# Layer 0 of a hybrid decoder trunk: the core's outputs are turned by VectorE in squares of 32 and put in place through DRAM

## The chip, the cores and the metric

The kernel runs on one core of a Trainium2 chip. The time is the device time of one execution in microseconds (us), the median of several runs. A profile of one execution gives the span from the first to the last instruction and every instruction's start, duration and waits.

## The reference

The kernel computes two layers of a decoder trunk on 1024 tokens of width 1024. Layer 0 is gated linear attention (GLA) in four heads, layer 1 is sparse attention. The change touches layer 0 alone. Its mixer, cut to what matters here:

```python
h = x @ w_in                                  # q, k, v, z, and the gate's low-rank input a
g = log_sigmoid(a @ w_a2 + b_a) / 16
...
o = o_intra + o_inter                         # within a chunk, and from the state S
o = o * rsqrt(mean(o * o, axis=-1) + 1e-5)    # per token and head, over 512 values
o = o.reshape(B, L, 2048) * gn_g
y = (o * silu(z)) @ w_out
...
x = layer_norm(ALPHA * x + y)                 # then a gated embedding is added
```

## The kernel before

**Halves, heads, chunks.** Layer 0 runs in two halves of 512 tokens; each half runs the four heads one after the other, and each head (a dictionary `u`, a "unit" of the planner) works in four chunks of 128 tokens. So there are 32 chunks with an output `o`. For each head the kernel makes the values (`v_phase`), queries and keys (`qk_phase`), and then the core: `core_steps` gives 16 steps, four for each chunk. `s1` makes the scores of a chunk and turns its keys, `s2` brings the state `R` forward, `s3` makes the chunk's output of three matmuls (with a state nine) in the PSUM bank `o`, and `s4` turns that output and gates it. Beside the core's steps run the bulk phases: the output projection of the head before (`out_phase`) and the gate projection of the next head (`z_phase`). The last head of a half has no z phase beside it, and its own output projection follows at once.

**Precision.** Matmuls are in fp32r with every operand split into a high and a low part: ScalarE writes the high part (`whi`, `uh`, L189 and L418), VectorE subtracts it from the value (`wlo`, `ul`, L191, L193 and L410). A product takes three matmuls of 512 columns. That goes for weights too, which come from DRAM into `wst` (L209) and are split up to two blocks ahead of their use (`Weights.step`).

**The turn.** `o` stands with tokens on the partitions (128 x 512). The output projection needs the head's 512 channels on the partitions, in four blocks `b` of 128, with the tokens along the row. In `s3`, VectorE copies `o` out of PSUM into `ot` (L729) and ScalarE sums its squares into `ss` (L731). In `s4`, TensorE turns the four 128 x 128 blocks of `ot` against an identity (L747, recorded at L62) into the PSUM bank `oT`, VectorE multiplies that by the gate `z` into `uf` (L757), and the product is split into `uh` and `ul` (L418, L410). GpSimd (POOL) makes the normalising factor `rs` of the chunk (L753, L755), which the projection's accumulation into `y` applies (L784).

**The order of the work.** The program is written out by a planner (`Flow`). It keeps a clock `now` that advances with each matmul it writes (512 columns count 0.213 us, a transpose 0.109 us), and a heap of jobs with due times on this clock: `after(dt, f)` puts one in, `chain` puts several behind each other, `spread` spaces a list evenly. A job that lacks something (`fl.req`) is put back by 0.3 us. `fl.need` runs jobs ahead of their times until a condition holds. The clock sets only the order in which instructions are written to each engine's queue; on the chip, each engine works through its queue in order and waits on semaphores. `spread(steps, fl.now, n * B + 15.5)` spaces a core's 16 steps, where `B` is 5.12 us and `n` the number of bulk blocks beside it: 8 for heads 1 and 2, and 4 for heads 0 and 3.

**Who waits for u.** `out_phase` takes `u["u"][t]` of its chunk `t` by `fl.need`, in the order of the chunks, with 12 matmuls on each. In heads 0 to 2 this is after the next head's `v_phase` and `qk_phase`; in head 3 it follows the core. `u["prev"]["out"]` counts the chunks that the previous head's projection has finished, after which their buffers `u` may be used again.

**The DMA queue.** All transfers are issued by SyncE (SP) from one queue, in the order written: weight loads (L209), and in the background, the weights of layer 1, which are loaded, split and stored in DRAM ahead of their use (`split_ahead`: L223, L235, L239, one step each 2.06 us of the planner's clock). In the other layer, `attend` already turns squares of 32 on VectorE (L1512), stores them in DRAM by four transfers (L1525) and loads them back (L1535).

Of the kernel before, what the change touches and what calls it, by code (L numbers as in the profile page):

```python
# [10 lines left out]
F32 = mybir.dt.float32  # L11
F32R = mybir.dt.float32r
# [4 lines left out]
AF = mybir.ActivationFunctionType  # L17
OP = mybir.AluOpType
# [7 lines left out]
GH = 4  # L26
ALPHA = 4.0 ** 0.25
EPS = 1e-5
# [19 lines left out]
class Flow:  # L48
# [20 lines left out]
    def after(self, dt, fn):  # L69
        self.at(self.now + dt, fn)  # L70

    def chain(self, *steps):

        (_, first), rest = steps[0], steps[1:]
        first()
        if rest:
            self.after(rest[0][0], lambda: self.chain((0, rest[0][1]), *rest[1:]))
# [200 lines left out]
def trunk_kernel(ctx, tc, x_tok, x_T, p_T, pos, freq, g_q, g_k, g_v, g_z, g_a, g_a2, g_ba, g_gn, g_o,  # L278
                 d_q, d_k, d_v, d_z, d_qi, d_ki, d_o, ln_gb, ple_c, gate_c, out):
    nc = tc.nc  # L280
    act, dve, pool = nc.scalar, nc.vector, nc.gpsimd
    fl = Flow(nc)
    mm, after, chain = fl.mm, fl.after, fl.chain
# [4 lines left out]
    dp = ctx.enter_context(tc.tile_pool(name="dp", bufs=1, space=bass.MemoryType.DRAM))  # L288
# [6 lines left out]
    lp = open_pool(layer0, "lp")  # L295
# [116 lines left out]
    def split(hi, lo, src, done=None):  # L412

        def second():
            lo_part(lo, src, hi)
            if done:
                done()
        chain((0, lambda: act.activation(hi, src, AF.Copy)), (0.9, second))  # L418
# [60 lines left out]
    def t2k(tag, dt=F32, bufs=8):  # L479
        return lp.tile([128, 512], dt, tag=tag, name=tag, bufs=bufs)  # L480
# [147 lines left out]
    def core_steps(u):  # L628
        h, half = u["h"], u["half"]
        fl.need(lambda: "qhl" in u and "D" in u)  # L630
        q, k, Dt, v = u["q"], u["k"], u["D"], u["v"]
        qh, ql = u["qhl"]
        u["ss"] = cp.tile([128, 4], F32, tag="ss", name="ss", bufs=2)
        u["rs"] = cp.tile([128, 4], F32, tag="rs", name="rs", bufs=2)
        st = {}

        def has_state(c):
            return not (half == 0 and c == 0)

        def makes_state(c):  # L640
            return not (u["last"] and c == 3)

        def make_S(c):
            parts = [[lp.tile([128, 512], F32R, tag=f"S{n}{d}", name="S") for n in "hl"] for d in range(2)]

            def high(d):
                return lambda: act.activation(parts[d][0], R[h][:, d], AF.Copy, scale=Dt[:, d, c:c + 1])

            def low(d):
                def f():  # L650
                    dve.scalar_tensor_tensor(parts[d][1], R[h][:, d], Dt[:, d, c:c + 1], parts[d][0].bitcast(F32),
                                             op0=OP.mult, op1=OP.subtract)
                    if d:
                        st["S", c] = parts
                        st["made", c] = True
                return f

            chain((0, high(0)), (0.6, high(1)), (0.5, low(0)), (0.6, low(1)))

        def s1(c):  # L660
            def f():
                cs = slice(c * 128, c * 128 + 128)
                if c == 0 and half:
                    make_S(0)
                tr = pp.tile([128, 4, 128], F32, tag="tr", name="tr")
                for d in range(2):
                    mm(tr[:, 0], k[:, d, cs], q[:, d, cs], d == 0, d == 1)
                if makes_state(c):
                    for d in range(2):
                        fl.transpose(tr[:, 1 + d], k[:, d, cs], ident)  # L670
                Af = Afs[c % 2]
                Ah = lp.tile([128, 128], F32R, tag="Ah", name="Ah", bufs=2)
                Al = lp.tile([128, 128], F32R, tag="Al", name="Al", bufs=2)
                kh = lp.tile([128, 2, 128], F32R, tag="kh", name="kh")
                kl = lp.tile([128, 2, 128], F32R, tag="kl", name="kl")

                def a():
                    dve.copy_predicated(Af, cmask, tr[:, 0])
                    if makes_state(c):
                        act.activation(kh, tr[:, 1:3], AF.Copy)  # L680

                def b():
                    if makes_state(c):
                        lo_part(kl, tr[:, 1:3], kh)
                        st["kt", c] = kh, kl
                    act.activation(Ah, Af, AF.Copy)

                def d_():
                    lo_part(Al, Af, Ah)
                    st["A", c] = Ah, Al  # L690
                    st["At", c] = fl.now
                chain((0, a), (0.6, b), (0.7, d_))
            return f

        def s2(c):
            def f():
                if not makes_state(c):
                    return
                fl.req(("kt", c) in st, v[c] is not None, not has_state(c) or ("made", c) in st)
                kh, kl = st.pop(("kt", c))  # L700
                vh, vl = v[c]
                for d in range(2):
                    ps = pp.tile([128, 512], F32, tag="U", name="U", bufs=2)
                    mm(ps, kh[:, d], vh, True, False)
                    mm(ps, kh[:, d], vl, False, False)
                    mm(ps, kl[:, d], vh, False, True)
                    if has_state(c):
                        dve.scalar_tensor_tensor(R[h][:, d], R[h][:, d], Dt[:, d, c:c + 1], ps,
                                                 op0=OP.mult, op1=OP.add)
                    else:  # L710
                        dve.tensor_copy(R[h][:, d], ps)
            return f

        def s3(c):
            def f():
                cs = slice(c * 128, c * 128 + 128)
                fl.req(("A", c) in st, v[c] is not None, not has_state(c) or ("S", c) in st)
                fl.ripe(st["At", c] + 1.6)
                Ah, Al = st.pop(("A", c))
                vh, vl = v[c]  # L720
                ps = pp.tile([128, 512], F32, tag="o", name="o")
                ops = [(Ah, vh), (Al, vh), (Ah, vl)]
                if has_state(c):
                    for d, (sh, sl) in enumerate(st.pop(("S", c))):
                        ops += [(qh[:, d, cs], sh), (ql[:, d, cs], sh), (qh[:, d, cs], sl)]
                for i, (l, r) in enumerate(ops):
                    mm(ps, l, r, i == 0, i == len(ops) - 1)
                ot = lp.tile([128, 512], F32, tag="ot", name="ot", bufs=2)
                dve.tensor_copy(ot, ps)  # L729
                junk = lp.tile([128, 512], BF16, tag="junk", name="junk")  # L730
                act.activation(junk, ps, AF.Square, accum_out=u["ss"][:, c:c + 1])  # L731
                st["o", c] = ot
                st["ot", c] = fl.now
                u["late"] = c == 3
                if c < 3:
                    after(0.3, lambda: make_S(c + 1))
            return f

        def s4(c):
            def f():  # L740
                cs = slice(c * 128, c * 128 + 128)
                fl.req(("o", c) in st, "z" in u, h == 0 or u["prev"].get("out", 0) > c)
                fl.ripe(st["ot", c] + 1.1)
                ot = st.pop(("o", c))
                ps = pp.tile([128, 4, 128], F32, tag="oT", name="oT")
                for b in range(4):
                    fl.transpose(ps[:, b], ot[:, b * 128:b * 128 + 128], ident)  # L747
                uf = lp.tile([128, 4, 128], F32, tag="uf", name="uf", bufs=2)
                uh, ul = t2k("u", F32R), t2k("u", F32R)

                def done():
                    rc = slice(c, c + 1)
                    pool.tensor_scalar(u["rs"][:, rc], u["ss"][:, rc], ALPHA ** 2 / 512.0, ALPHA ** 2 * EPS,  # L753
                                       op0=OP.mult, op1=OP.add)
                    pool.tensor_tensor(u["rs"][:, rc], u["rs"][:, rc], mhalf[:, rc], op=OP.pow)  # L755
                    u["u"][c] = uh, ul
                chain((0, lambda: dve.tensor_mul(uf, ps, u["z"][:, :, cs])),  # L757
                      (0.8, lambda: split(uh, ul, uf.rearrange("p b t -> p (b t)"), done)))
            return f

        return fl.ordered([s1(0), s2(0), s3(0), s1(1), s4(0), s2(1), s3(1), s1(2), s4(1), s2(2), s3(2), s1(3), s4(2),
                           s2(3), s3(3), s4(3)])

# [1075 lines left out]
```

## Time and profile before

| | |
|---|---|
| Median of 3 runs | 1962.26 us (1962.2 to 1963.73) |
| Span of the profiled execution | 1962.1 us |
| Instructions | 26826 |
| Layer 0, about | 0 to 1020 us |
| Copies of `o` out of PSUM (L729) | 32, from 88.3 to 940.0 us |
| Transposes of `ot` on TensorE | 128, from 92.2 to 941.4 us |
| Gate products (L757) | 32, from 94.2 to 941.8 us |

The profiled execution's own time isn't listed apart from the runs; its span lies 0.2 us below their median. The profile's engines are PE (TensorE's matmuls), PEld (its weight loads, which overlap the matmuls), DVE (VectorE), ACT (ScalarE), POOL (GpSimd) and SP. `out<-in` names the tiles that an instruction writes and reads. A line such as L58 or L410 can be a helper's, so groups are told apart by tiles. `<-` behind an idle time names what ended it. The chain of work that ended last is followed back from the last instruction; an engine that fills the chain sets the time.

### The profile page before, as it was taken

How to read it: one execution, taken by the hardware profiler on the slowest of the kernel's cores; microseconds unless marked ns; L12 is line 12 of the kernel's file. 1: busy time of each engine (PE TensorE's matmuls, PEld its weight loads, DVE VectorE, ACT ScalarE, POOL GpSimd, SP SyncE). 2: the span in 40 equal slices, each digit the busy share in tenths (PEclk: the TensorE clock that was granted, in tenths of full speed). 3: DMA queues.
4: the chain of work that ended last, by engine and by line, in shares of the span. 5: the costliest groups of instructions: out<-in, count | busy, mean ns of one | idle time of the engine just before them, and what ended most of it. 6: DMA issues, size and time to landing. Idle time of an engine off the chain costs nothing.

```text
span 1962.1 us, 26826 instructions
## 1 busy us (share of the span) xinstructions
PE 1948.5 (99%) x9060; PEld 1614.2 (82%) x9060; DVE 1490.0 (76%) x3039; ACT 1021.7 (52%) x1928; POOL 53.6 (3%) x115
## 2 busy tenths in 40 slices
PE   9999999999999999999999999999999999999999
PEld 7888888888888888888888888888878888888877
DVE  5776676687778887877858987768797987777873
ACT  5664646446465646464545676766443553434432
POOL 0000000010000000000100000000000000000000
PEclk9999999999999999999999999999999999999999
DMA  4566565668757656656676588877866998888874
GB/s 153 185 184 212 190 215 181 215 183 263 249 186 236 210 194 195 211 180 209 209 260 250 181 309 289 275 264 267 317 216 234 362 317 295 297 302 276 291 272 145
DMA packets 174218, 464.96 MB, mean 237 GB/s; under 512 B 20096, under 2 KB 21120, under 8 KB 167936
## 3 DMA queue, kind: packets, MB, share of 16 engines
q1 hardware_dynamic: 174080, 463.25, 70.6%
q8 instruction: 71, 1.16, 0.2%
q14 instruction: 67, 0.55, 0.1%
HBM read 331.18 MB, written 131.99 MB: 236 GB/s over the span
## 4 chain that ended last, share of the span: by engine, by line
PE 93%; DVE 3%; ACT 2%; issue 1%; DMA 0%; SPq 0%; DVEq 0%; ACTq 0%
PE pb L58 70%; PE o L58 8%; PE U L58 6%; PE S L58 6%; PE oT L62 1%; PE tr L58 1%; DVE bn L828 0%; DVE y L786 0%; PE S L62 0%; ACT x L885 0%; DMA y<-in_x_T 0%; PE pb L62 0%; DVE sc L1067 0%; PE tr L62 0%; PE xt L62 0%
## 5 line engine op out<-in xcount | busy, mean ns | idle before, releaser
L58 PE MATMUL pb<-x,whi 128*128 128x512 f32 x2272 | 707.2, 392 | 0.0
L58 PEld LDWEIGHTS pb<-x,whi 128*128 128x128 f32 x2272 | 417.1, 188 | 79.5 <-DVE x L410 0.4
L58 PE MATMUL pb<-x,wlo 128*128 128x512 f32 x1136 | 443.1, 390 | 0.0
L58 PE MATMUL pb<-whi,u 128*128 128x512 f32 x1024 | 342.3, 394 | 0.1
L58 PEld LDWEIGHTS pb<-x,wlo 128*128 128x128 f32 x1136 | 213.3, 188 | 46.2 <-DVE wlo L191 0.4
L58 PEld LDWEIGHTS pb<-whi,u 128*128 128x128 f32 x1024 | 192.4, 188 | 40.8 <-ACT u L418 0.5
L58 PE MATMUL pb<-wlo,u 128*128 128x512 f32 x512 | 200.5, 392 | 0.0
L191 DVE TENSOR_TENSOR wlo<-wst,whi 128x512 fp32r<-128x512 f32 x232 | 154.5, 686 | 44.2 <-ACT whi L189 43.8
L189 ACT ACTIVATE whi<-wst 128x512 fp32r<-128x512 f32 x232 | 136.5, 622 | 81.7 <-DMA wst<-in_g_k 28.4
L1506 ACT ACTIVATE sq<-P,mx 128x128 f32<-128x128 f32 (+7 forms) x128 | 99.0, 774 | 89.3 <-DVE mx L1499 54.1
L1552 ACT ACTIVATE ph<-PT 128x512 fp32r<-128x512 f32 (+1 forms) x160 | 93.9, 601 | 63.5 <-PE o L58 44.6
L58 PE MATMUL S<-kT,q 128*128 128x512 f32 (+2 forms) x576 | 121.8, 343 | 0.0
L1550 DVE TENSOR_TENSOR PT<-PT,ph 128x512 fp32r<-128x512 f32 (+1 forms) x160 | 102.3, 649 | 17.7 <-ACT ph L1552 17.2
L58 PEld LDWEIGHTS S<-kT,q 128*128 128x128 f32 x576 | 100.5, 188 | 17.8 <-DVE mx L1499 0.7
L58 PEld LDWEIGHTS pb<-wlo,u 128*128 128x128 f32 x512 | 96.3, 188 | 18.8 <-DMA wlo<-wls 0.3
L1133 ACT ACTIVATE tk<-sc,tki 128x768 f16<-128x768 f32 (+2 forms) x90 | 92.8, 1031 | 22.9 <-DVE tki L1142 19.1
L58 PE MATMUL o<-ph,vT 128*128 128x512 f32 (+2 forms) x384 | 103.2, 353 | 0.2 <-ACT ph L1552 0.2
L1512 DVE STREAM_TRANSPOSE sq<-sq 128x128 f32<-128x128 f32 (+7 forms) x128 | 97.9, 769 | 4.0 <-ACT sq L1506 3.7
L731 ACT ACTIVATE junk<-o 128x512 bf16<-128x512 f32 x32 | 19.1, 597 | 152.1 <-DVE ot L729 141.0
L237 DVE TENSOR_TENSOR pst<-pst,phi 128x512 fp32r<-128x512 f32 x130 | 89.3, 687 | 5.4 <-ACT phi L233 5.0
L58 PE MATMUL pb<-whi,x 128*128 128x512 f32 x256 | 86.2, 395 | 0.4 <-DVE x L410 0.4
L58 PE MATMUL U<-whi,x 128*128 128x512 f32 x256 | 84.9, 391 | 0.0
(318 smaller groups left out, 3362.0 us busy)
## 6 DMA issues: line engine op xcount, KB each, us to landing
whi<-whs SPq DMA_DIRECT2D x128, 512.0 KB
wlo<-wls SPq DMA_DIRECT2D x128, 512.0 KB
sqd<-sq SPq DMA_DIRECT2D x192, 256.0 KB
PT<-sqd SPq DMA_DIRECT2D x48, 1024.0 KB
whs<-phi SPq DMA_DIRECT2D x130, 256.0 KB
wls<-pst SPq DMA_DIRECT2D x130, 256.0 KB
wst<-in_g_z SPq DMA_DIRECT2D x32, 512.0 KB
wst<-in_g_o SPq DMA_DIRECT2D x32, 512.0 KB
```

The lines of the kernel that those rows point to most:

```text
L58: self.pe.matmul(out, lhsT, rhs, start=start, stop=stop)
L62: self.pe.transpose(out, in_, ident)
L189: self.nc.scalar.activation(hi[:, c], st[:, c], AF.Copy, scale=1.0 if gain is None else gain)
L191: self.nc.vector.tensor_sub(lo[:, c], st[:, c], hi[:, c].bitcast(F32))
L237: self.nc.vector.tensor_sub(st, st.bitcast(F32), hi.bitcast(F32))
L731: act.activation(junk, ps, AF.Square, accum_out=u["ss"][:, c:c + 1])
L1133: act.activation(junk()[:, :n], scs[j], AF.Sign, bias=cand[:, j:j + 1].bitcast(F32), accum_out=cnt[:, j:j + 1])
L1506: act.activation(to, rows, AF.Exp, scale=-1.0, bias=mx, accum_out=sm[:, t:t + 1])
L1512: dve.transpose(x, x)
L1550: dve.tensor_sub(lo, lo.bitcast(F32), hi.bitcast(F32))
L1552: chain((0, lambda: act.activation(hi, lo.bitcast(F32), AF.Copy)), (0.8, second))
```

## The change

For 30 of the 32 chunks (`by_square`: all but chunk 3 of head 3, in each half) TensorE no longer turns the output. VectorE's copy out of PSUM becomes a transpose of 32 x 32 squares (`dve.transpose`), which writes `ot` with the squares of each block side by side. 2.2 us later on the planner's clock, `squares_out` stores `ot` in a DRAM tile `od` by four DMAs, one for each group of 32 partitions, so that the squares come to stand in their places; 4.0 us later `squares_in` loads it into `uf` by one DMA; 4.0 us after that, `gate` multiplies by `z` in place and splits the product, with views that put the columns in order. `made` holds what `done` held before. In `s4` nothing is left for these chunks. Chunk 3 of head 3 keeps its path.

```diff
@@ -726,7 +726,11 @@
                 for i, (l, r) in enumerate(ops):
                     mm(ps, l, r, i == 0, i == len(ops) - 1)
                 ot = lp.tile([128, 512], F32, tag="ot", name="ot", bufs=2)
-                dve.tensor_copy(ot, ps)
+                if by_square(c):
+                    dve.transpose(ot.rearrange("p (m b i) -> p b m i", m=4, b=4), ps)
+                    after(2.2, lambda: squares_out(c, ot))
+                else:
+                    dve.tensor_copy(ot, ps)
                 junk = lp.tile([128, 512], BF16, tag="junk", name="junk")
                 act.activation(junk, ps, AF.Square, accum_out=u["ss"][:, c:c + 1])
                 st["o", c] = ot
@@ -736,8 +740,50 @@
                     after(0.3, lambda: make_S(c + 1))
             return f
 
+        def by_square(c):
+            return h < GH - 1 or c < 3
+
+        def squares_out(c, ot):
+            od = dp.tile([4, 32, 4, 128], F32, tag="od", name="od", bufs=4)
+            for a in range(4):
+                nc.sync.dma_start(od[:, :, a].rearrange("m r x -> r m x"),
+                                  ot[32 * a:32 * a + 32].rearrange("p (m x) -> p m x", m=4))
+
+            def squares_in():
+                fl.req(h == 0 or u["prev"].get("out", 0) > c)
+                uf = lp.tile([128, 512], F32, tag="uf", name="uf", bufs=2)
+                nc.sync.dma_start(uf, od.rearrange("m r a x -> (m r) (a x)"))
+                after(4.0, lambda: gate(c, uf))
+            after(4.0, squares_in)
+
+        def gate(c, uf):
+            fl.req("z" in u)
+            turned = uf.rearrange("p (a b i) -> p b a i", a=4, b=4)
+            uh, ul = t2k("u", F32R), t2k("u", F32R)
+
+            def part(x):
+                return x.rearrange("p (b a i) -> p b a i", b=4, a=4)
+
+            def high():
+                act.activation(part(uh), turned, AF.Copy)
+
+            def low():
+                dve.tensor_sub(part(ul), turned, part(uh).bitcast(F32))
+                made(c, uh, ul)
+            z = u["z"][:, :, c * 128:c * 128 + 128].rearrange("p b (a i) -> p b a i", a=4)
+            chain((0, lambda: dve.tensor_mul(turned, turned, z)), (0.8, high), (0.9, low))
+
+        def made(c, uh, ul):
+            rc = slice(c, c + 1)
+            pool.tensor_scalar(u["rs"][:, rc], u["ss"][:, rc], ALPHA ** 2 / 512.0, ALPHA ** 2 * EPS,
+                               op0=OP.mult, op1=OP.add)
+            pool.tensor_tensor(u["rs"][:, rc], u["rs"][:, rc], mhalf[:, rc], op=OP.pow)
+            u["u"][c] = uh, ul
+
         def s4(c):
             def f():
+                if by_square(c):
+                    return
                 cs = slice(c * 128, c * 128 + 128)
                 fl.req(("o", c) in st, "z" in u, h == 0 or u["prev"].get("out", 0) > c)
                 fl.ripe(st["ot", c] + 1.1)
@@ -748,14 +794,8 @@
                 uf = lp.tile([128, 4, 128], F32, tag="uf", name="uf", bufs=2)
                 uh, ul = t2k("u", F32R), t2k("u", F32R)
 
-                def done():
-                    rc = slice(c, c + 1)
-                    pool.tensor_scalar(u["rs"][:, rc], u["ss"][:, rc], ALPHA ** 2 / 512.0, ALPHA ** 2 * EPS,
-                                       op0=OP.mult, op1=OP.add)
-                    pool.tensor_tensor(u["rs"][:, rc], u["rs"][:, rc], mhalf[:, rc], op=OP.pow)
-                    u["u"][c] = uh, ul
                 chain((0, lambda: dve.tensor_mul(uf, ps, u["z"][:, :, cs])),
-                      (0.8, lambda: split(uh, ul, uf.rearrange("p b t -> p (b t)"), done)))
+                      (0.8, lambda: split(uh, ul, uf.rearrange("p b t -> p (b t)"), lambda: made(c, uh, ul))))
             return f
 
         return fl.ordered([s1(0), s2(0), s3(0), s1(1), s4(0), s2(1), s3(1), s1(2), s4(1), s2(2), s3(2), s1(3), s4(2),
```

## The prediction, before the result was known

> **What bounds the kernel now.** First the page: busy time, and the chain that ended last.
>
> ```profile
> PE 1948.5 (99%) x9060; PEld 1614.2 (82%) x9060; DVE 1490.0 (76%) x3039; ACT 1021.7 (52%) x1928; POOL 53.6 (3%) x115
> PE 93%; DVE 3%; ACT 2%; issue 1%; DMA 0%; SPq 0%; DVEq 0%; ACTq 0%
> q1 hardware_dynamic: 174080, 463.25, 70.6%
> ```
>
> TensorE never rests, and the chain runs on it for 93% of the span. So the time is the sum of what TensorE executes plus a few small waits. Busy time over-counts pipelined matmuls; the chain doesn't, so I price TensorE work by the chain. Next, the core stages of layer 0 by windows:
>
> ```profile
> core 0: us, PE busy (x) PEld busy (x) DVE busy (x) ACT busy (x) POOL busy (x), PEclk, DMA share, GB/s
> 85.00:125.00 40.00, 40.00 (x194) 33.15 (x193) 29.29 (x52) 22.20 (x48) 2.97 (x8) 1.00 0.57 195
> 760.00:820.00 60.00, 60.00 (x274) 49.86 (x273) 51.61 (x121) 30.46 (x57) 0.74 (x2) 1.00 0.67 210
> 880.00:942.00 62.00, 61.27 (x286) 49.97 (x285) 50.38 (x89) 27.68 (x55) 2.93 (x8) 1.00 0.66 207
> ```
>
> TensorE is full. VectorE has a quarter of its time free in the first half and some 14 to 19% in the second; ScalarE has about half. The granted clock is full, so nothing comes from there. Where TensorE does wait in the second half (570 to 970 us), the waits are short:
>
> ```profile
> PEld o L58 <- DVE Al L410: 2.1, 4, 0.9
> PEld oT L62 <- DVE ot L729: 0.3, 1, 0.3
> ```
>
> **The change, part by part.**
>
> *Removed: four TensorE transposes in each of 30 units* (16 units in each half, less the last head's last chunk). By tile, and in the chain's pieces from 84.81 us on:
>
> ```profile
> L62 PE MATMUL oT<-ident,ot x128: 270/272/329, 92.2 to 941.4; 128*128 128x128 f32 x128
> 92.34 0.44 PE oT L62 x4
> 102.36 0.44 PE oT L62 x4
> 119.64 0.44 PE oT L62 x4
> ```
>
> One lasts 272 ns, but four advance the chain by 0.44 us, 0.11 us each, because they overlap. 30 x 0.44 = 13.2 us of TensorE go, and no other TensorE work takes their place. This is the whole gain, 0.7%.
>
> The Trainium skill ("VectorE: DVE Perf Modes", Rules for kernel authors) speaks against this: a 128x128 transpose belongs on TensorE if a PSUM destination will do, while 32x32 blocks are VectorE's. "TensorE: Matmul & The Clock Gate" (Part 4) gives about 275 ns for one in a kernel. The 272 ns row agrees, but the chain shows 0.11 us as its cost; by the page's figure the estimated gain would be 33 us.
>
> *Replaced: the copy out of PSUM becomes a square transpose; the gate's product reads SBUF.* By form:
>
> ```profile
> L729 DVE COPY ot<-o 128x512 f32<-128x512 f32 x32 | 22.1, 691 | 35.1 <-PE o L58 34.9
> L1512 DVE STREAM_TRANSPOSE sq<-sq 128x512 f32<-128x512 f32 x16 | 11.3, 707 | 3.6 <-ACT sq L1506 3.6
> L1512 DVE STREAM_TRANSPOSE sq<-sq 128x1024 f32<-128x1024 f32 x16 | 19.7, 1234 | 0.0
> L410 DVE TENSOR_TENSOR v<-pb,v 128x512 fp32r<-128x512 f32 x16 | 11.0, 689 | 9.7 <-ACT v L418 9.7
> L410 DVE TENSOR_TENSOR x<-y,x 128x512 fp32r<-128x512 f32 x24 | 16.3, 683 | 4.8 <-ACT x L418 4.8
> L757 DVE TENSOR_TENSOR uf<-oT,z 128x512 f32<-128x512 f32 x32 | 22.0, 686 | 3.6 <-PE oT L62 3.6
> L1607 DVE TENSOR_TENSOR uf<-o,z 128x512 f32<-128x512 f32 x32 | 22.1, 691 | 68.4 <-PE o L58 68.1
> ```
>
> The trace has square transposes from SBUF alone: 0.71 us at this size. A PSUM source adds 6 ns elsewhere (`v<-pb` against `x<-y`), so I take 0.71; bounds are the plain copy, 0.69, and the transpose of twice the width, 1.23. Per unit VectorE gains 0.02 us (0 to 0.54), over 30 units 0.5 us (0 to 16), beside TensorE in stages where it has 14% or more free. If that cover were gone, this would be the price. The gate's product now walks runs of 32; L1607 does that already at 0.69 us, as L757 before. The split's two halves stay one ScalarE and one VectorE instruction, and POOL's two small ones only move behind them, so these come out at nothing. The Square on ScalarE still follows VectorE on that bank.
>
> *Added: five DMAs a unit on SP's queue*, four writes of 64 KB in runs of 512 B and one load of 256 KB. Layer 1 makes the same trip:
>
> ```profile
> 1092.67 2.72 SPq L1525 DMA_DIRECT2D sqd<-sq  x4
> 1504.09 7.14 SPq L1525 DMA_DIRECT2D sqd<-sq  x8
> 369.67 0.33 SPq L239 DMA_DIRECT2D wls<-pst  x1
> 371.81 0.33 SPq L223 DMA_DIRECT2D pst<-in_d_o  x1
> 414.64 1.05 SPq L807 DMA_DIRECT2D pt<-in_p_T  x2
> 419.25 1.31 ACT L418 ACTIVATE ah<-pt 128x512 fp32r<-128x512 f32 x2 [2.31 <-DMA pt<-in_p_T]
> SPq L223 <- DMA wls<-pst: 32.2, 19, 5.7
> ```
>
> Four writes take SP 2.7 us (3.6 by the row of eight). A write's landing: L223 waits for the write of L239 and goes 2.1 us after it (the waits of SP run to 5.7 us). A load: ScalarE waits for `pt` until 4.6 us after the issue began. So the round trip from the transposed tile is about 2.7 + 1.5 + 0.4 + 3.6 = 8.2 us, counting the last write's landing from the middle of its issue. The planner puts the store 2.2 us behind the products, the load 4.0 later, the gate 4.0 later: 10.2 us, with the transpose inside the first 2.2. So the gate finds its tile with about 1 us to spare, and some gates will wait a little.
>
> Who stands behind the waits: behind the load on SP, which waits for the four writes, stand the weight loads (L209) and the split-ahead traffic (L223, L235, L239). Their blocks are split up to two ahead of TensorE, two times 24 matmuls or some 11 us, which covers a wait of 2 us. Behind the product on VectorE stand weight remainders, y's accumulation and the next chunk's parts; ScalarE's high part waits for the product, with the weights' high parts behind it. In heads 1 and 2 the planner spreads 16 steps over 56.5 us, so a chunk's products follow the last ones by 14 us and their parts are made by the third step between, ahead of the gate: I cost these waits at 0 there. In a half's last head (16 steps over 36 us) the steps are closer, and I take 0.5 us a half, 1 us in all; bounds are 0 and one of today's longest such waits (0.9 us) in each of 30 units, 27 us.
>
> The transfers are 30 x 512 KB, 3% of the queue's bytes, and 30 x 640 packets, 11% of its packets: 2 to 8 points on 70.6%. Not the bound.
>
> *Moved: u is ready later.* For three heads its reader, the output projection, runs only after the next head's value, query and key projections (192 matmuls). For the last head it follows at once, and chunk 2 is the critical one:
>
> ```profile
> 403.69 0.70 DVE L729 COPY ot<-o 128x512 f32<-128x512 f32 x1
> 934.14 0.69 DVE L729 COPY ot<-o 128x512 f32<-128x512 f32 x1
> 940.56 0.68 DVE L410 TENSOR_TENSOR u<-uf,u 128x512 fp32r<-128x512 f32 x1
> 412.76 28.58 PE pb L58 x126
> 941.72 27.25 PE pb L58 x120
> ```
>
> The projection starts at 412.8 and 941.7 us and asks for chunk 2 after 24 matmuls of 0.227 us (28.58/126), 5.4 us on; the three units of that head taken away make it 1.3 us earlier: 416.8 and 945.8. Chunk 2 is turned from 403.7 and 934.1 on; 10.2 us to the gate and 2.4 us for product and split (0.8 and 0.9 of the planner's, then 0.69) make 416.3 and 946.7. Today's value at 934.14 became u at 941.2. So half 0 just holds and half 1 waits 0.9 us; with VectorE's queue late by a microsecond I take 2 us for both (0 to 10, if each trip takes 4 us more).
>
> *The planner's clock* counts 0.109 us a transpose, so 13 us less pass by it, and the background that splits layer 1's weights (a step each 2.06 us) has up to six steps left at the end of layer 0. Its last store stands close to that end already:
>
> ```profile
> 1012.70 0.32 SPq L239 DMA_DIRECT2D wls<-pst  x1
> 1017.54 5.76 SPq L1317 DMA_DIRECT2D x2s<-x  x2
> 1023.39 0.89 SPq L1644 DMA_DIRECT2D kI<-kv_s  x2
> L233 ACT ACTIVATE phi<-pst 128x512 fp32r<-128x512 f32 x130 | 80.5, 619 | 1.5 <-DMA pst<-in_d_o 0.8 <-DMA pst<-in_d_q 0.5 <-DMA pst<-in_ple_c 0.2
> L237 DVE TENSOR_TENSOR pst<-pst,phi 128x512 fp32r<-128x512 f32 x130 | 89.3, 687 | 5.4 <-ACT phi L233 5.0 <-ACT junk L731 0.3
> ```
>
> Two pieces made in a burst lie beside the projections that TensorE then runs; I cost them at 0, and uncovered at 2 x (0.62 + 0.69) = 2.6 us.
>
> **Sum.** 13.2 - 1.0 - 2.0 = 10.2 us off the profiled span of 1962.1 gives 1951.9; the median of the runs, 1962.26, lies 0.2 above that span, so the prediction is **1952.1 us**.
>
> **Rivals.**
>
> *A wait takes the place of the transposes.* If the trip through DRAM is 4 us longer than I add up, the last head's projection waits some 5 us in each half and the gates add a microsecond or two: 13.2 - 12 gives 1961, no change. For it: SP's wait of 5.7 us, the issue row of eight. Against: the 2.1 us row, and DMA engines free for a third of the time.
>
> *Slower: the product blocks VectorE.* It sits in VectorE's queue before its tile has landed, and everything behind it stops. It decides above 0.44 us of TensorE time lost per unit, the size of the gain. At 1 us a unit: 1962.1 - 13.2 + 30 + 2 = 1981. For it: VectorE is 80% busy in the second half, and in the last head the chain already passes through it. Against: TensorE's waits there are 2.4 us in 400 today, and the gate lies after the next chunk's parts.
>
> *The transposes cost what they last.* If each took 272 ns from TensorE, 120 x 0.272 - 3 = 30 us would go: 1932. Against: consecutive groups of four move the chain by 0.44, each time. The page named above gives this figure.
>
> *The planner doesn't do it:* if the projection's demand forced the queued steps out early, they would only sit in their queues and wait, which is the first rival.
>
> **How the numbers follow.** Forecast (1948.5 to 1955.5, its waits at 0 or twice what I take) 0.62; longer waits that leave a part of the gain (1955.5 to 1958.3) 0.08; no change 0.17; slower 0.11; the durations' full price 0.02. A measurement here can tell about 0.2%, 3.9 us, from no change, so faster is 0.72, same 0.17, slower 0.11. The range runs from 1948.5, all waits at nothing, to 1962.0, which takes in the first rival; it leaves out the slower case and the full price.
>
> **What would show it.** Right: `oT` falls to 8 transposes, L58's matmuls are as many as before, a STREAM_TRANSPOSE of 0.69 to 0.75 us stands where L729 did, and the stages of the heads shrink by 1.76 us each (1.3 in the last). Wrong: a transpose out of PSUM near 1.2 us; VectorE's product waiting for `uf` by DMA for more than 2 us each; TensorE's weight loads waiting for `u` at the start of the last projection by more than 3 us; or waits for `wlo` that aren't there today.

## The result, and the profile after

| | median, us | ratio to the kernel before, 95% interval |
|---|---|---|
| before (4 runs) | 1962.23 | |
| changed (4 runs, 1949.73 to 1954.55) | 1951.86 | 0.9945 (0.9933 to 0.9957) |

The change took 10.4 us off; 10.2 were forecast. By the interval it took 8.4 to 13.1 us. (The two profiled executions differ by 9.3 us in span; that of the changed kernel is the slowest of its four.) First the page of the changed kernel: busy times, the chain that ended last, the DMA queue.

```profile
PE 1934.1 (99%) x8940; PEld 1602.4 (82%) x8940; DVE 1490.6 (76%) x3039; ACT 1020.6 (52%) x1928; POOL 55.3 (3%) x115
PE 89%; DVE 5%; ACT 3%; DMA 2%; issue 1%; SPq 0%; DVEq 0%; ACTq 0%
q1 hardware_dynamic: 195680, 478.99, 73.3%
```

120 matmuls fewer, TensorE still 99% busy, VectorE's busy time the same to a microsecond, and the queue's share up by 2.7 points. The chain is on TensorE for less of the span, because it now meets waits whose history leads back through other engines. The waits are read by themselves below. Next, by tile, what turns `o` (duration in ns: min/median/max; start of the first and the last).

```profile
L730 DVE STREAM_TRANSPOSE ot<-o x30: 708/716/718, 86.4 to 918.4; 128x512 f32<-128x512 f32 x30
L749 SPq DMA_DIRECT2D od<-ot x120: 318/440/1322, 87.2 to 920.5; - x120
L755 SPq DMA_DIRECT2D uf<-od x30: 319/322/449, 94.4 to 924.3; - x30
L62 PE MATMUL oT<-ident,ot x8: 270/272/328, 403.8 to 929.2; 128*128 128x128 f32 x8
```

A square transpose out of PSUM lasts 0.716 us, 0.025 more than the copy whose place it takes. The chain through a core stage (start, length, what) now has nothing where four transposes of 0.44 us stood between the matmuls:

```profile
306.52 0.44 PE tr L58 x4
306.96 0.22 PE tr L62 x2
307.18 6.83 PE pb L58 x30
314.01 1.36 PE U L58 x6
```

The heads' stages shrink about as forecast. In half 0, the copies of each head's first `o` start at 88.28, 174.70, 279.22 and 380.23 us before, and the transposes in their place at 86.42, 171.02, 273.21 and 372.38 us. From one head to the next that is 1.8, 2.3 and 1.8 us less; 1.76 was forecast.

The profiled executions also differ where the change has no part: the first of these times lies 1.86 us apart, with no `o` turned yet. So a second measure takes the core stages alone, in each profile: from half 0's first `o` to the first transpose of `xt` (`y`, turned at the end of each half), and from half 1's first `o` to the last transpose of `xt`. Before and after, the transposes of `xt` and half 1's first `o`:

```profile
L62 PE MATMUL xt<-ident,y x64: 270/272/273, 441.2 to 976.3; 128*128 128x128 f32 x64
617.42 0.69 DVE L729 COPY ot<-o 128x512 f32<-128x512 f32 x1 [0.88 <-PE o L58]
...
L62 PE MATMUL xt<-ident,y x64: 270/272/273, 435.4 to 965.1; 128*128 128x128 f32 x64
613.04 0.72 DVE L730 STREAM_TRANSPOSE ot<-o 128x512 f32<-128x512 f32 x1 [0.88 <-PE o L58]
```

The two stretches took 352.9 and 358.9 us before, 711.8 in sum, and 349.0 and 352.1 after, 701.1 in sum: 10.7 us less. Between them lie 176.2 us before and 177.6 after, so a part of this may be lost again there; e5 below has 177.1, and whether the change has a part in it stays open.

What TensorE's weight loads wait for (us in total, times, longest): the two longest groups before, in 85 to 450 us; then the changed kernel, in 85 to 450 us (three lines) and 570 to 970 us (two); then VectorE's wait for the load from DRAM, and SP's wait for the four stores:

```profile
PEld U L58 <- ACT kh L680: 0.8, 2, 0.5
PEld U L58 <- DVE kl L410: 0.7, 2, 0.5
...
PEld pb L58 <- DVE u L771: 2.5, 1, 2.5
PEld oT L62 <- DVE ot L733: 0.5, 1, 0.5
PEld pb L58 <- DVE ql L410: 0.5, 1, 0.5
...
PEld o L58 <- DVE Al L410: 1.3, 2, 1.1
PEld pb L58 <- DVE u L771: 1.1, 1, 1.1
...
DVE uf L774 <- DMA uf<-od: 4.0, 4, 1.4
...
SPq L755 <- DMA od<-ot: 11.8, 9, 3.2
```

The new waits are the two for `u` (L771), one at the start of each half's last projection: 3.6 us. All other such waits in these two stretches fell, from 4.5 us to 2.3. Only four of 30 gates waited for their load, 4.0 us in all. Why `u` is late in half 0 shows in VectorE's order of time around it:

```profile
405.76 0.69 DVE L774 TENSOR_TENSOR uf<-uf,z 128x512 f32<-128x512 f32 x1 [0.60 <-DMA uf<-od]
406.37 0.74 DVE L193 SCALAR_TENSOR_TENSOR wlo<-wst,gn,whi 128x512 fp32r<-128x512 f32 x1
407.03 0.74 DVE L824 SCALAR_TENSOR_TENSOR y<-pb,rs,y 128x512 f32<-128x512 f32 x1
407.81 0.69 DVE L868 BATCH_NORM_STATS2 bn<-y 128x6 f32<-128x512 f32 x1
408.42 0.74 DVE L193 SCALAR_TENSOR_TENSOR wlo<-wst,gn,whi 128x512 fp32r<-128x512 f32 x1
409.07 0.69 DVE L237 TENSOR_TENSOR pst<-pst,phi 128x512 fp32r<-128x512 f32 x1
409.67 0.69 DVE L410 TENSOR_TENSOR u<-uf,u 128x512 fp32r<-128x512 f32 x1
410.27 0.69 DVE L771 TENSOR_TENSOR u<-uf,u 128x512 fp32r<-128x512 f32 x1
```

And ScalarE's high part of the same chunk:

```profile
406.67 0.62 ACT L768 ACTIVATE u<-uf 128x512 fp32r<-128x512 f32 x1
```

The product of chunk 2 (L774) waited 0.6 us for its load, but then its low part (L771) stood behind six other instructions, with chunk 3's low part (L410, 409.67) among them. It began 3.0 us after the high part had ended (407.29).

### The profile page after: what moved, and what is told of

It is laid out like the page before. It is cut to its first block, busy times and chain, and to the rows that moved or that the text cites. A ratio compares the mean times of both kernels' runs of the same rounds, so it can differ in the third digit from the quotient of the medians.

```text
span 1952.8 us, 26780 instructions
## 1 busy us (share of the span) xinstructions
PE 1934.1 (99%) x8940; PEld 1602.4 (82%) x8940; DVE 1490.6 (76%) x3039; ACT 1020.6 (52%) x1928; POOL 55.3 (3%) x115
## 3 DMA queue, kind: packets, MB, share of 16 engines
q1 hardware_dynamic: 195680, 478.99, 73.3%
## 4 chain that ended last, share of the span: by engine, by line
PE 89%; DVE 5%; ACT 3%; DMA 2%; issue 1%; SPq 0%; DVEq 0%; ACTq 0%
PE pb L58 66%; PE o L58 8%; PE U L58 6%; PE S L58 6%; PE tr L58 1%; DVE bn L868 1%; DVE y L826 0%; PE S L62 0%; DMA sqd<-sq 0%; ACT x L925 0%; ACT whi L189 0%; DVE wlo L191 0%; DMA y<-in_x_T 0%; DVE sc L1107 0%; DMA xst<-x2s 0%
## 5 line engine op out<-in xcount | busy, mean ns | idle before, releaser
L237 DVE TENSOR_TENSOR pst<-pst,phi 128x512 fp32r<-128x512 f32 x130 | 88.9, 684 | 7.5 <-ACT phi L233 7.4
```

The lines of the kernel that those rows point to most:

```text
L237: self.nc.vector.tensor_sub(st, st.bitcast(F32), hi.bitcast(F32))
```

## The experiments

Each time stands beside the runs of the kernel before on the same chip (medians 1962.5 to 1962.6 us); the changed kernel is taken as 1951.9. Runs of one kernel spread by 1.4 to 6 us, so a difference of 1 us between two medians shows nothing. So the sum of the two core stretches described above stands beside the median of each kernel; it comes from one execution of each:

| | median of the runs, us | two core stretches in the profile, us |
|---|---|---|
| before | 1962.2 to 1962.6 | 711.8 |
| changed | 1951.9 | 701.1 |
| e4 | 1965.91 | 714.3 |
| e5 | 1962.6 | 711.8 |
| e6 | 1954.15 | 702.4 |
| e7 | 1963.25 | 710.3 |
| e2 | 1950.04 | 698.1 |
| e10 | 1949.71 | 698.0 |
| e1 | 1949.95 | 697.8 |
| e9 | 1951.27 | 698.3 |
| e3 | 1956.09 | 704.0 |
| e8 | 1957.83 | 704.7 |

The rest of the span took 1248.5 to 1252.0 us in these executions. That is as much spread as many of the differences below.

**e4: the transposes put back, with nobody reading them.**

```diff
 if by_square(c):
+    ps = pp.tile([128, 4, 128], F32, tag="oT", name="oT")
+    for b in range(4):
+        fl.transpose(ps[:, b], ident, ident)
     return
```

> The changed kernel, and in step s4 of the 30 chunks TensorE transposes the identity four times into the bank oT, which nobody reads: TensorE has the 120 transposes back, all else is as changed. Theory (the gain is TensorE's time alone): 13.2 us more than the changed kernel, 1965, so the new path's waits show as 3 us above the kernel before. Rival (most of the gain is from s4's waits on VectorE and PSUM): less than 7 us more. Rival (a transpose costs the 272 ns that it lasts): 33 us more, 1985.

Measured: 1965.91 us, ratio 1.0017 (1.0008 to 1.0025), 14.0 us above the changed kernel. By tile, the 120 stand there with their old duration:

```profile
L62 PE MATMUL oT<-ident x120: 270/272/274, 91.5 to 932.5; 128*128 128x128 f32 x120
```

14.0 / 120 = 0.117 us each, not the 0.272 that one lasts; by the core stretches 13.2 / 120 = 0.110. So the gain goes with TensorE's transposes: the rival of less than 7 us is refuted too, and the rest of the new path costs 3.3 us against the kernel before (1.6 to 4.9 by the interval; 2.5 by the core stretches). The edit also gives the planner's clock its 0.109 us for each transpose back. So it returns the old order of the work together with TensorE's time, and doesn't tell the two apart; that the sum comes out at the chain's 0.11 us each speaks for TensorE's time.

**e5: the added transfers alone**, in the kernel before.

```diff
 dve.tensor_copy(ot, ps)
+if by_square(c):
+    after(2.2, lambda: squares_out(c, ot))
...
+    back = lp.tile([128, 512], F32, tag="uf", name="back", bufs=2)
+    nc.sync.dma_start(back, od.rearrange("m r a x -> (m r) (a x)"))
```

> The kernel before, and for the same 30 chunks the four stores of ot to DRAM and the load back into a buffer that nobody reads (it takes turns with the gate's own buffers): the added transfers alone, with TensorE still turning. Theory (SP and the DMA engines have room): within 2 us of the kernel before, 1962. Rival (SP's queue and the transfers delay weights): 1 us for each chunk or more, over 1990.

Measured: 1962.6 us, ratio 1.0001 (0.9992 to 1.001). From 85 to 450 us, by windows, before and in e5 (TensorE's, its weight loads', VectorE's, ScalarE's and POOL's busy time; clock, DMA share, GB/s):

```profile
85.00:450.00 365.00, 364.88 (x1697) 302.37 (x1696) 258.01 (x455) 192.92 (x359) 19.23 (x41) 1.00 0.63 200
85.00:450.00 365.00, 364.91 (x1697) 302.52 (x1697) 258.37 (x455) 192.73 (x359) 19.28 (x41) 1.00 0.69 222
```

The DMA engines go from 0.63 to 0.69, SP has five more issues a chunk, and TensorE loses nothing; the core stretches are the same to 0.1 us. The transfers by themselves are free here, within the 2 us of the interval; what they can cost is a wait behind them.

**e6: each square transpose made twice.**

```diff
-dve.transpose(ot.rearrange("p (m b i) -> p b m i", m=4, b=4), ps)
+for _ in range(2):
+    dve.transpose(ot.rearrange("p (m b i) -> p b m i", m=4, b=4), ps)
```

> The changed kernel with each of the 30 square transposes made twice: 30 x 0.72 = 21.5 us more on VectorE, nothing else. Theory (VectorE's time is covered beside TensorE, but for the last heads, where its queue is what u waits for): 1 to 5 us more than the changed kernel. Rival (VectorE is as good as full in these stages, so what it gets shows): 15 to 21 us more.

Measured: 1954.15 us, ratio 0.9959 (0.9946 to 0.9971), 2.3 us above the changed kernel for 21.5 us more work:

```profile
L731 DVE STREAM_TRANSPOSE ot<-o x60: 705/717/719, 86.1 to 920.1; 128x512 f32<-128x512 f32 x60
```

The intervals of the two kernels overlap; the core stretches give 1.3 us more. So some nine tenths of VectorE's added time is covered, and the rival, 15 us or more, is refuted. A transpose out of PSUM of twice the length, the upper bound of the prediction, would still have left most of the gain.

**e7: VectorE made to wait for the load.**

```diff
-after(4.0, lambda: gate(c, uf))
+after(1.0, lambda: gate(c, uf))
```

> The changed kernel with the gate put 1.0 instead of 4.0 us of the planner's clock behind the load, so VectorE's product waits for the landing, by the mean trip some 2 to 3 us for each of 30 chunks, 60 to 90 us of VectorE's waiting in all. This puts a price on the forecast's slower case. Theory (heads 0 to 2 take such a wait without loss, the last heads lose a little): 1 to 6 us more than the changed kernel. Rival (VectorE blocked is TensorE blocked): 0.5 to 1 us a chunk, 15 to 30 us more.

Measured: 1963.25 us, ratio 1.0007 (0.9998 to 1.0015), 11.4 us above the changed kernel, between the two expectations. VectorE's wait for the load from 85 to 970 us, and TensorE's longest groups of waits (two from 85 to 450 us, then three from 570 to 970 us):

```profile
DVE uf L774 <- DMA uf<-od: 55.6, 23, 4.7
...
PEld U L58 <- DVE m L525: 2.2, 1, 2.2
PEld U L58 <- ACT kh L680: 2.1, 2, 1.7
...
PEld U L58 <- DVE m L525: 2.9, 3, 1.0
PEld o L58 <- DVE Al L410: 2.4, 3, 1.1
PEld pb L58 <- DVE wlo L191: 1.9, 1, 1.9
```

55.6 us of waiting on VectorE became 11.4 us of the kernel's time, a fifth. (The 55.6 us are from the fastest of the eleven runs, 2.6 us below the median; in that run the core stretches are 9.2 us longer than the changed kernel's, a sixth.) It reaches TensorE at many places: the core's parts, the gate of the next head (L525), weights. So the forecast's slower case is a true mechanism: three microseconds less room between load and gate, on the planner's clock, take the whole gain away by the medians and most of it by the core stretches.

**e2, e10: the low part sooner in the last heads**, and in e10 the gate sooner too.

```diff
-... (0.8, high), (0.9, low))
+... (0.8, high), (0.9 if h < GH - 1 else 0.2, low))
 # e10 has this too:
-after(4.0, lambda: gate(c, uf))
+after(4.0 if h < GH - 1 else 3.0, lambda: gate(c, uf))
```

> In the last heads the low part is written 0.2 instead of 0.9 us of the planner's clock behind the high part, so ahead of other work in VectorE's queue. Theory (u is late because its low part stands in VectorE's queue for 2.6 to 3.0 us after the high part is there): TensorE's waits for u at the last projections fall from 2.5 and 1.1 us to under 1 in sum, time about 1949.5, 2.5 us below the changed kernel. Rival (u is late because the trip through DRAM is long): the waits stay, 1952.

> e2 and in the last heads the gate 3.0 instead of 4.0 us behind the load. Theory (u is late in VectorE's queue; in e2 the product of chunk 2 didn't wait for its load): the remaining waits for u (1.1 and 0.5 us) go, 1949. Rival (the load lands just as the gate is due): the product waits for its load, and TensorE's waits move to the core's parts: 1950 to 1951.5.

Measured: e2 1950.04 us, ratio 0.9933 (0.992 to 0.9945); e10 1949.71 us, ratio 0.9936 (0.9923 to 0.995). TensorE's waits for `u` in e2, one in each half:

```profile
PEld pb L58 <- DVE u L771: 1.1, 1, 1.1
...
PEld pb L58 <- DVE u L771: 0.5, 1, 0.5
```

They fell from 3.6 to 1.6 us, the median by 1.8 and the core stretches by 3.0. So the low part's place in the queue was one cause of the wait. e10 has the same two waits, 1.1 and 0.5 us, so its theory, that they would go, is wrong; its time and its core stretches are those of e2.

**e1, e9: chunk 2 of the last heads stays on TensorE too**, in e9 with e2's edit.

```diff
-return h < GH - 1 or c < 3
+return h < GH - 1 or c < 2
```

> Chunks 2 and 3 of each half's last head go by TensorE, 28 chunks by squares. Theory (the gain is 0.44 us of TensorE a chunk, and 3.6 us of it are given back where the last projection waits for chunk 2): 28 x 0.44 = 12.3 us off, no wait for u at the projection's start: about 1950 against 1952 for the changed kernel, 2.7 us better (3.6 won, 0.9 of transposes back). Rival (the projection waits for something else at that place anyway): 0.9 us worse than the changed kernel, 1953.

> e1 and e2 together: chunks 2 and 3 of the last heads by TensorE, and the low part of chunks 0 and 1 written 0.2 us behind the high part. Theory: e1 has no wait for u left, so nothing is added: 1950 (1949.5 to 1950.5). Rival (the two gains are separate): 1948.2.

Measured: e1 1949.95 us, ratio 0.9934 (0.9921 to 0.9948); e9 1951.27 us, ratio 0.9942 (0.993 to 0.9955). e1 has no wait for `u` left and is 1.9 us below the changed kernel, of 2.7 expected; by the core stretches it is 3.3. In e9 the second edit adds nothing, as expected of it. Its median is 1.3 us above that of e1 and outside the 1949.5 to 1950.5 expected, which the spread covers; its core stretches are 0.5 us longer.

**e3, e8: the last heads all by TensorE**, and in e8 their split later.

```diff
-return h < GH - 1 or c < 3
+return h < GH - 1
 # e8 has this too, in s4:
-(0.8, lambda: split(...))
+(4.0 if c < 2 else 0.8, lambda: split(...))
```

> Only heads 0 to 2 go by squares, 24 chunks; the last heads are as before the change. Theory: 24 x 0.44 = 10.6 us off and no wait for u: 1951.7, the same as the changed kernel, since its last six chunks win 2.6 and lose about 3. Rival (all chunks give the same): 24/30 of 10.4 us, 1953.9.

> The kernel of e3 (last heads by TensorE), with the split of u for chunks 0 and 1 of the last heads put 4.0 instead of 0.8 us behind the product. In e3 TensorE waits 2.5 us in half 0 and 2.1 us in half 1 for Al, and the high and low parts of u stand ahead of Al's two parts in the queues of ScalarE and VectorE. Theory (squares in the last heads win because they take that split out of the core's tight order): the waits for Al fall by 1 to 2 us in sum, 1954.5. Rival (the waits come from the weights' and the background's steps in the order): 1956, unchanged.

Measured: e3 1956.09 us, ratio 0.9963 (0.9951 to 0.9976), 4.2 us above the changed kernel, where the theory had no difference and the rival 2.0; by the core stretches it is 2.9 us above. So the theory fails, and the rival fits within the spread. e8 1957.83 us, ratio 0.9975 (0.9965 to 0.9985). In e3 other waits stand in the last heads, in half 0 and in half 1:

```profile
PEld o L58 <- DVE Al L410: 2.5, 1, 2.5
...
PEld o L58 <- DVE Al L410: 2.1, 2, 1.6
PEld oT L62 <- DVE ot L733: 0.6, 1, 0.6
```

The theory counted those heads as free of waits without squares; they aren't. In e8 the waits for `Al` are 2.8 us from 85 to 450 us and 3.1 us from 570 to 970 us. But e8 doesn't test its theory, for its edit didn't move the split out of the way. VectorE's order of time around the long wait of half 0, in the kernel before, in e3 and in e8:

```profile
399.66 0.28 DVE L410 TENSOR_TENSOR Al<-Af,Ah 128x128 fp32r<-128x128 f32 x1
401.77 0.69 DVE L237 TENSOR_TENSOR pst<-pst,phi 128x512 fp32r<-128x512 f32 x1
...
391.38 0.69 DVE L237 TENSOR_TENSOR pst<-pst,phi 128x512 fp32r<-128x512 f32 x1 [1.83 <-ACT phi L233]
391.98 0.69 DVE L410 TENSOR_TENSOR u<-uf,u 128x512 fp32r<-128x512 f32 x1
394.57 0.28 DVE L410 TENSOR_TENSOR Al<-Af,Ah 128x128 fp32r<-128x128 f32 x1
...
390.92 0.69 DVE L237 TENSOR_TENSOR pst<-pst,phi 128x512 fp32r<-128x512 f32 x1 [1.83 <-ACT phi L233]
391.52 0.69 DVE L410 TENSOR_TENSOR u<-uf,u 128x512 fp32r<-128x512 f32 x1
394.11 0.28 DVE L410 TENSOR_TENSOR Al<-Af,Ah 128x128 fp32r<-128x128 f32 x1
```

In e8 the low part of `u` stands ahead of `Al` just as in e3. In half 1 its low part even came nearer to `Al`, from 923.52 to 926.68 us with `Al` at 928.6 and 928.5, and the wait there rose from 1.6 to 2.4 us. What the lines do show for half 0 is the background's step (L237): before, it stood behind `Al`; in e3 and e8 it stands ahead, and VectorE waits 1.83 us for its high part `phi`. With its own 0.6 us of the queue that is the whole wait that e3 has more than the kernel before there, 2.5 against 0.2 us. This speaks for e8's rival, the steps of the background in the order; it is read from one execution each, and no run moved that step alone. What the split adds in half 1 stays open.

## Why the prediction was right, point by point

**The removed transposes.** 13.2 us by the chain's pieces of 0.44; e4 measures 14.0, and 13.2 by the core stretches. The rival by which a transpose costs its duration is refuted by the same run (33 expected). The Trainium skill, "TensorE: Matmul & The Clock Gate" (Part 4), gives about 275 ns in a kernel, measured there on bf16: the 272 ns in the rows, of fp32, agree as a duration, but in this kernel's full queue four follow each other within 0.44 us. Its rule in "VectorE: DVE Perf Modes" (Rules for kernel authors), TensorE for 128x128, does not hold for this kernel's time, 1951.86 against 1962.23 us: TensorE is the full engine, and squares with a trip through DRAM win.

**The square transpose.** 0.71 us was taken, 0.716 measured; covered, by e6, to some nine tenths even when doubled.

**The trip and its waits.** The forecast had the gate find its tile with about 1 us to spare and some gates waiting. Four of 30 waited, and with 3.0 us less room the 23 gates that waited did so for 2.4 us each (55.6/23), so by this estimate their room was 0.6 us in the mean. SP's four stores took 4 x 0.44 = 1.8 us by their median, where 2.7 was taken. The transfers and SP's issues cost nothing that shows, by e5. The bounds, nothing to 27 us, were right to be wide: e7 lies at 11.4. The 1 us taken for TensorE's waits on the core's parts isn't there: without those for `u`, its waits in the two stretches fell by 2.2 us.

**The last heads.** 2 us were taken for the waits for `u`; the profile shows 3.6. Half 0 was to just hold and waited 2.5, half 1 was to wait 0.9 and waited 1.1. The microsecond allowed for VectorE's queue was too small in half 0: the low part stood 3 us behind the high part. The forecast named 3 us of such waits as a sign of being wrong: neither half reaches that, the two together do. So the losses forecast, 3.0 us, stand against 3.3 in e4 (2.5 by the core stretches), but they are made up otherwise: 1.6 us more for `u`, and 2.2 us less at the core's other waits where 1 us more was forecast. The gain's mechanism was right. That the sum comes within 0.2 us is in part luck; a difference that small is less than the runs can tell.

**The planner's clock.** The burst of the background at the end of layer 0 was costed at nothing, rightly. By windows of the changed kernel, TensorE is busy throughout that stretch:

```profile
970.00:1020.00 50.00, 50.00 (x223) 41.12 (x222) 28.83 (x47) 21.09 (x37) 1.81 (x1) 1.00 0.86 284
```

But the forecast looked for the clock's effect at that end alone. By e3's lines, a step of the background that comes to stand elsewhere inside a head can cost some 2 us.

**Some steps of the forecast were loose.** It took the profiled span of before, 1962.1, as 0.2 us below the median's execution. In the changed kernel the profiled execution took 1954.55 us with a span of 1952.8, so 1.75 us lie around a span, and the profiled execution of before was likely the slowest shown, 1963.73. The difference of the two medians hides it. The bounds of its waits at nothing or twice what it takes come to 1949.1 and 1955.1 us by its own terms, not 1948.5 and 1955.5. And a chunk's transfers are 720 packets by the two pages, (195680 - 174080) / 30, not 640.

**A better version.** e1, e2 and e10 lie about 2 us below the changed kernel, but their intervals overlap with its own. By the core stretches, in one execution each, they are 3.0 to 3.3 us shorter than the changed kernel. That they are faster than the kernel before is shown, that they beat the change is likely.

## What to carry to other kernels

Where one engine is full, price what is taken from it by how far it moves the chain, not by its duration: here 0.11 us of 0.27. Work given to engines with room is free only as long as its results come before anyone asks: look for the reader that follows most closely, and at the place that the last small instruction gets in its engine's queue. A wait for a DMA in a compute engine's queue costs others too, here a sixth to a fifth of its length. Where an order is planned by a clock, taking work out moves other work too, so read the order again. And before an experiment is read, see in its trace that the edit moved what it was meant to move.

## What was not expected

21.5 us more of work on VectorE cost 2.3 us (e6), about a tenth and not clear of the spread, and 55.6 us of waiting on it cost 11.4 (e7), a fifth. The work comes in pieces of 0.72 us, the waits in pieces of up to 4.7; that this makes the difference is not shown. And the last heads, taken back to TensorE, cost 2.9 us by the core stretches (e3). Their 24 transposes are 2.6 us of that by e4's 0.110 us each: the waits for `u` that go, 3.6 us, are made up by new ones for `Al`.
